# Query stacks rewritten in place by halves, gate-a tiles computed inside their own head pair, and five banks for filling

## The chip, the cores and the metric

The kernel runs on one core of a Trainium2 chip. The metric is the device time of one execution in microseconds (us). TensorE (PE) does the matrix products into eight PSUM banks, VectorE (DVE), ScalarE (ACT) and GpSimd (POOL) do the rest, and SyncE (SP) starts the loads.

## The reference

Two layers over 1088 token columns: 1024 of a prompt and 64 of a sample that continues a cache of 512 keys. Layer 0 runs attention over the 256 best keys of an indexer (8 heads of 64, two key/value heads) beside a short gated convolution. Layer 1 is a gated spatial mixer. Cut to the part that the change touches:

```python
q, k, v, ga, qi, ki, wi, gb, gc, xin, gz = _split(h @ w_in, EVEN_SPLITS)
...                      # top-k of the indexer's scores, masked logits
p = jax.nn.softmax(logits, axis=-1)
o = jnp.einsum('bqgrk,bqkgd->bqgrd', p, vg)
a_out = o * jax.nn.silu(ga)
...                      # short convolution: y
b_out = gb * y * jax.nn.silu(gz)
out = jnp.concatenate([a_out, b_out], axis=-1) @ w_out
```

## The kernel before

**Layout.** Activations lie with features on the partitions and the 1088 columns along the free axis. A projection tile is 128 output features: three chunks of columns (`CHUNKS`, 364, 364 and 360), each 24 matmuls (8 input tiles, times high by high, low by high and high by low parts), so 72 matmuls. A weight tile is loaded into one of two ring slots and split into a rounded high part by ACT (L238) and a low part by POOL (L239); `fetch()` starts this for the next tile when a tile begins, and the slot comes free when the tile before has been used.

**Attention of layer 0.** The eight heads are four pairs `t` = 0 to 3; `self.q[:, t, :]` holds a pair's queries and is overwritten by its output. For each pair `pair_stack` (L691) writes two query stacks of 128 partitions (high parts on one half by ACT, L698, low parts on the other by POOL, L699), whole, into tiles that are allocated anew for each pair. Then `attend` (L711) handles the blocks of 128 queries in the order of `ORDER`: block b has 128 x (b + 1) keys. Blocks 0 and 1 use a constant mask; the others use `bias`, which `mask` (L593 to L607) writes on DVE just before the attention. `softmax` computes logits in chunks of at most 512 keys (PE L620), adds the mask and takes the extremum (DVE L622), Exp (ACT L625), reciprocal (DVE L626) and division (POOL L627). `weighted` transposes the probabilities (PE L650), splits them into high and low parts (ACT L276, DVE L277) and multiplies them with the values (PE L658), in groups of two key blocks; the result goes back to q (ACT L662, DVE L722). `attend_sample` does the same for the 64 sample columns (L727, L732). Logits use PSUM banks of tag lg (three), transposes pt (two), sums av (one).

**Filling.** The projections that are left at that point are done as filling, one matmul per step: Q tiles 1 to 3, GB tiles 0 to 3 (product on DVE, L894), GA tiles 0 to 3 (gate a). `steps` (L250) is the generator, with the two banks of tag pj. The first `BEFORE` = 435 steps stand ahead of the attention. After that `pace` (L200) adds steps behind a matmul of the attention: `RATE` gives the number after a chunk of logits, after a group of weighted sums and after a group of transposes. A step may not be issued before the matmul that it was added behind. A GA tile waits until its pair is done (`self.done <= t`, L922); until then a step does nothing. So GA0 fills pair 1, GA1 pair 2, GA2 pair 3, and GA3 stands behind the last pair. `gate_a` copies a chunk to SBUF (L909), applies Silu to the whole tile after the third (L911) and multiplies it into q on POOL (L912); for t = 3 it does so chunk by chunk (L905, L906).

**Order.** Each engine runs its own queue in order. The order in the queues is made when the program is built, by a planner that follows the program's text where it can and lets later, ready instructions go ahead (`schedule_with_timeline_sim=True`). Afterwards q and bo are split into `ah` and `al` by chunks of columns (`OUT_CHUNKS`), and `out_projection` runs 8 tiles of 24 matmuls for each chunk, through `product`. The weights of its first two tiles use the two ring slots; the others get memory that attention has used.

Of the kernel before, what the change touches and what calls it, by code (L numbers as in the profile page):

```python
# [17 lines left out]
P = 128  # L18
# [17 lines left out]
NCH = 3  # L36
CW = 448


# [44 lines left out]
SPANS = [slice(min(COL[j] for j in g[0]), max(COL[j] for j in g[0]) + 1) for g in GROUPS]  # L84
ORDER = [(0, 1, 2, 3, 4, 5, 6, 7)] + [(7, 0, 6, 1, 5, 2, 4, 3)] * 3


BEFORE = 435
RATE = ((1, 1, 2),) * 4

# [7 lines left out]
class Trunk:  # L98
# [150 lines left out]

    def steps(self, w, evac, chunks=range(NCH), n=2, tag="pj"):  # L250

        hi, lo = w
        k = 0
        for c in chunks:
            a, b = CHUNKS[c]
            ps = self.bank(tag, "pj")[:, 0:b - a]
            for kt in range(KT):
                for i, (wt, at) in enumerate(((hi, self.ah), (hi, self.al), (lo, self.ah))):
                    if k and k % n == 0:
                        yield  # L260
                    k += 1
                    self.nc.tensor.matmul(ps, wt[:, kt, :], at[:, kt, a:b], start=kt == 0 and i == 0,  # L262
                                          stop=kt == KT - 1 and i == 2)
            evac(c, ps)
# [425 lines left out]

    def pair_stack(self, pool, t):  # L691

        nc = self.nc
        st = [pool.tile([P, TC], F32R, tag=f"qst{e}", name="qst") for e in range(2)]
        for a, b in ((0, 512), (512, TC)):
            for e in range(2):
                x, h, l = self.q[64 * e:64 * e + 64, t, a:b], slice(64 * e, 64 * e + 64), slice(64 - 64 * e, P - 64 * e)
                nc.scalar.activation(st[e][h, a:b], x, AF.Copy)  # L698
                nc.gpsimd.tensor_sub(st[e][l, a:b], x, st[e][h, a:b])  # L699
        return st  # L700

# [8 lines left out]

    def attend(self, pool, st, t, b):  # L711
        n = P * (b + 1)
# [10 lines left out]

    def attend_sample(self, pool, st, t):
        both = pool.tile([P, P], F32R, tag="qs", name="qs", bufs=1)
# [36 lines left out]
    def layer0(self):  # L762
# [41 lines left out]
        with ExitStack() as es:  # L804
# [74 lines left out]
            with self.pool("attn", "right") as ap:  # L879
# [8 lines left out]
                ap.tile([P, 512], F32R, tag="pth", name="place", bufs=2)  # L888
                for e in range(2):
                    ap.tile([P, TC], F32R, tag=f"qst{e}", name="place")  # L890

# [7 lines left out]
                def gate_a(t):  # L899
                    def evac(c, ps):  # L900
                        if c == 0:
                            ga[:] = [ap.tile([P, TC], F32, tag="ga", name="ga")]
                        g, q = ga[0], self.q[:, t, :]
                        if t == 3:
                            nc.scalar.activation(g[:, cols(c)], ps, AF.Silu)  # L905
                            nc.vector.tensor_mul(q[:, cols(c)], q[:, cols(c)], g[:, cols(c)])  # L906
                            return

                        nc.scalar.activation(g[:, cols(c)], ps, AF.Copy)  # L909
                        if c == NCH - 1:  # L910
                            nc.scalar.activation(g, g, AF.Silu)  # L911
                            nc.gpsimd.tensor_mul(q, q, g)  # L912
                    return evac

                evacs = {Q_: lambda t: into(self.q[:, t, :]), GB: gate_b, GA: gate_a}
                left = list(ATTN_TILES)
                self.done = 0

                def tiles():
                    while left:  # L920
                        kind, t = left[0]
                        while kind == GA and self.done <= t:  # L922
                            yield
                        key, w = ahead.pop(0)
                        assert key == (kind, t)
                        fetch()
                        yield from self.steps(w, evacs[kind](t), n=1)
                        left.pop(0)
                        yield

                self.side = tiles()
                for _ in range(BEFORE):
                    next(self.side)
                for t in range(4):
                    while (Q_, t) in left:
                        next(self.side)
                    self.rate = RATE[t]
                    st = self.pair_stack(ap, t)
                    for b in ORDER[t]:
                        self.attend(ap, st, t, b)  # L940
                    if t == 0:
                        self.sample_keys(ap)
                    self.attend_sample(ap, st, t)
                    self.done = t + 1
# [3 lines left out]
            for chunk in OUT_CHUNKS:  # L948
                s = slice(*chunk)
                for t in range(4):  # L950
                    for k, src in ((4 + t, self.bo), (t, self.q)):
                        self.split(self.ah[:, k, s], self.al[:, k, s], src[:, t, s])

# [7 lines left out]
    def out_projection(self, l, ws, after):  # L961
# [4 lines left out]
        for c in range(NCH):  # L966
# [4 lines left out]
            for t in range(KT):  # L971
                ps = self.bank(tags[0], "op")
                tags = tags[1:] + tags[:1]
                self.product(ps[:, 0:w], ws[t], a0, b0)
                for j, a, b in self.spans(c):
# [245 lines left out]
```

## Time and profile before

| | us |
|---|---|
| median of 3 runs | 1156.94 (1156.66 to 1160.60) |
| the profiled execution | 1157.27 |
| its span on the core | 1155.5 |
| filling without attention, DVE at top-k and masks | 344.8 to 424.8 |
| pairs 0 to 3 (first logits to the last write of the sample's columns) | 424.8, 481.9, 530.3, 581.3, 632.9 |
| output projection of layer 0 and layer 1 | from 634.8 |

Page and views name instructions by engine, line and tile. A busy PE includes matmuls that overlap, so a matmul's cost is read from the distance of starts; PEclk is the granted share of the TensorE clock, whose two levels are 2.4 and 1.2 GHz.

### The profile page before, as it was taken

Reading aid. Unit: us, or ns where it says so; the run is one execution under the profiler, and the core shown is the slowest. Engines: PE = TensorE matmul, PEld = TensorE weight load, DVE = VectorE, ACT = ScalarE, POOL = GpSimd, SP = SyncE. Lnnn points to the kernel's source line nnn. Section 1 sums busy time; section 2 is a strip of 40 time slices with the busy share of each in tenths; the row PEclk is TensorE's granted clock in tenths of the full one; section 3 lists DMA queues with packets and bytes.
Section 4 is the critical chain, followed back from the end, with each engine's and each line's share of the span. In section 5 each row is a group of like instructions: output and inputs, shape, how many; then the busy total and the mean of one; then the engine's idle time right before and its main releaser. Section 6 shows DMA issues by size and latency. Waiting matters only on the chain.

```text
span 1155.5 us, 18886 instructions
## 1 busy us (share of the span) xinstructions
PE 1100.1 (95%) x7255; PEld 1051.7 (91%) x7255; DVE 670.9 (58%) x1657; ACT 516.8 (45%) x976; POOL 442.6 (38%) x454
## 2 busy tenths in 40 slices
PE   4899999999999979999898999999999999999997
PEld 4789689999999968888797999999999999999996
DVE  5712799998886998776666424411186064247134
ACT  5233686856777147777757313511221211135111
POOL 2633223466547165354523136521133211154222
PEclk9999999999999989998999999999999999999999
DMA  9746411211101110000000801011112111131012
GB/s 362 305 156 215 179 29 56 91 40 38 37 19 56 37 46 10 20 1 19 19 1 19 281 2 40 35 55 37 37 57 82 37 37 37 38 109 37 1 65 91
DMA packets 26074, 81.84 MB, mean 71 GB/s; under 512 B 3072, under 2 KB 9984, under 8 KB 23552
## 3 DMA queue, kind: packets, MB, share of 16 engines
q1 hardware_dynamic: 25984, 80.63, 19.8%
q8 instruction: 57, 0.93, 0.3%
q14 instruction: 33, 0.27, 0.1%
HBM read 74.50 MB, written 6.12 MB: 70 GB/s over the span
## 4 chain that ended last, share of the span: by engine, by line
PE 79%; DVE 8%; ACT 5%; issue 3%; POOL 2%; DMA 2%; SPq 0%; POOLq 0%; DVEq 0%; ACTq 0%
PE pj L247 40%; PE op L247 16%; PE pj L262 8%; PE av L658 3%; PE p_ps L650 2%; PE logit_ps L620 2%; PE ada_ps L153 2%; PE score_ps L427 1%; PE sgu_ps L1036 1%; PE first L318 1%; DVE cum L604 1%; PE score_ps L428 1%; POOL w_lo L239 1%; POOL hf L329 1%; ACT S L625 1%
## 5 line engine op out<-in xcount | busy, mean ns | idle before, releaser
L247 PE MATMUL pj<-ah,w_hi 128*128 128x364 f32 (+1 forms) x984 | 326.0, 331 | 1.0 <-ACT w_hi L238 1.0
L247 PE MATMUL pj<-al,w_hi 128*128 128x364 f32 (+1 forms) x984 | 323.8, 329 | 0.0
L247 PE MATMUL pj<-ah,w_lo 128*128 128x364 f32 (+1 forms) x984 | 323.1, 329 | 0.0
L239 POOL TENSOR_TENSOR w_lo<-w_raw,w_hi 128x1024 fp32r<-128x1024 f32 x63 | 159.1, 2527 | 351.2 <-ACT w_hi L238 350.8
L247 PEld LDWEIGHTS pj<-ah,w_hi 128*128 128x128 f32 x984 | 185.0, 188 | 2.0 <-ACT w_hi L238 1.3
L247 PEld LDWEIGHTS pj<-ah,w_lo 128*128 128x128 f32 x984 | 184.8, 188 | 0.3 <-issue 0.2
L247 PEld LDWEIGHTS pj<-al,w_hi 128*128 128x128 f32 x984 | 185.1, 188 | 0.0
L238 ACT ACTIVATE w_hi<-w_raw 128x1024 fp32r<-128x1024 f32 x69 | 72.9, 1058 | 135.7 <-PE pj L247 83.2
L247 PE MATMUL op<-ah,w_lo 128*128 128x448 f32 (+2 forms) x384 | 126.5, 330 | 3.0 <-POOL w_lo L239 3.0
L247 PE MATMUL op<-ah,w_hi 128*128 128x448 f32 (+2 forms) x384 | 127.1, 331 | 0.9 <-ACT ah L276 0.5
L247 PE MATMUL op<-al,w_hi 128*128 128x448 f32 (+2 forms) x384 | 126.4, 329 | 0.7 <-DVE al L277 0.7
L528 DVE TENSOR_SCALAR_CACHE_REDUCE cum<-S,cand 128x512 bf16<-128x512 f32 (+5 forms) x142 | 119.1, 838 | 2.0
L262 PE MATMUL pj<-ah,w_hi 128*128 128x364 f32 (+1 forms) x288 | 96.0, 333 | 6.6 <-DVE bo L894 5.6
L262 PE MATMUL pj<-al,w_hi 128*128 128x364 f32 (+1 forms) x288 | 96.4, 335 | 0.0
L262 PE MATMUL pj<-ah,w_lo 128*128 128x364 f32 (+1 forms) x288 | 95.7, 332 | 0.0
L976 DVE SCALAR_TENSOR_TENSOR x<-op,mod,x 128x192 f32<-128x192 f32 (+2 forms) x64 | 30.4, 497 | 104.9 <-PE op L247 102.5
L555 ACT ACTIVATE junk<-S,cand 128x896 bf16<-128x896 f32 (+2 forms) x78 | 77.7, 996 | 24.3 <-DVE m L558 20.5
L627 POOL TENSOR_SCALAR S<-S,sm 128x384 f32<-128x384 f32 (+8 forms) x68 | 50.4, 748 | 87.2 <-DVE sm L626 64.9
L247 PEld LDWEIGHTS op<-ah,w_lo 128*128 128x128 f32 x384 | 73.0, 190 | 5.5 <-POOL w_lo L239 3.3
L247 PEld LDWEIGHTS op<-ah,w_hi 128*128 128x128 f32 x384 | 73.0, 190 | 3.5 <-ACT ah L276 0.9
L247 PEld LDWEIGHTS op<-al,w_hi 128*128 128x128 f32 x384 | 73.0, 190 | 3.3 <-DVE al L277 1.1
L984 POOL TENSOR_TENSOR acc<-acc,sq 128x448 f32<-128x448 f32 (+2 forms) x40 | 39.2, 979 | 94.4 <-ACT sq L982 93.6
(242 smaller groups left out, 2001.3 us busy)
## 6 DMA issues: line engine op xcount, KB each, us to landing
w_raw<-in_w SPq DMA_DIRECT2D x53, 512.0 KB, 3.4
ada<-in_ada_w SPq DMA_DIRECT2D x19, 1024.0 KB, 9.1
w_raw<-in_wo SPq DMA_DIRECT2D x16, 512.0 KB, 3.5
x<-in_x SPq DMA_DIRECT2D x8, 544.0 KB, 6.6
bo<-in_ada_w SPq DMA_DIRECT2D x4, 1024.0 KB, 6.9
x<-in_x SPq DMA_DIRECT2D x1, 1792.0 KB, 9.5
out_y<-x SPq DMA_DIRECT2D x1, 1792.0 KB, 6.6
x<-in_x SPq DMA_DIRECT2D x1, 1536.0 KB, 9.4
```

Source lines behind the costliest of these rows:

```text
L153: nc.tensor.matmul(pt[32 * g:32 * g + 32, 0:P], self.cs[:, kt, :], raw(kt)[:, g * P:(g + 1) * P], start=kt == 0, stop=kt == KT - 1, tile_p ...
L238: nc.scalar.activation(hi, raw, AF.Copy)
L239: (nc.gpsimd if lo_eng == "pool" else nc.vector).tensor_sub(lo, raw, hi)
L247: last = self.nc.tensor.matmul(ps, wt[:, kt, :], at[:, kt, c0:c1], start=n == 0, stop=n == len(mms) - 1)
L262: self.nc.tensor.matmul(ps, wt[:, kt, :], at[:, kt, a:b], start=kt == 0 and i == 0, stop=kt == KT - 1 and i == 2)
L528: V.tensor_scalar(junks[0][:, 0:SW[j]], self.S[:, span(j)], thr, 0.0, op0=OP.is_lt, op1=OP.add, accum_out=col(cv, j))
L555: nc.scalar.activation(junks[1][:, 0:SW[j]], self.S[:, span(j)], AF.Sign, scale=-1.0, bias=col(cand, j), accum_out=col(cv, j))
L620: mm = nc.tensor.matmul(pt[:, 0:w], lhs, keys[i][:, g, s], start=i == 0, stop=i == 1)
L627: nc.gpsimd.tensor_scalar(p, p, st[:, 3:4], 0.0, op0=OP.mult, op1=OP.add)
L658: mm = nc.tensor.matmul(av[:, 0:m], self.vs[0:r, vbase + j, g, :], t[0:r, o:o + m], start=j == 0 and i == 0, stop=j == nj - 1 and i == 1)
L976: nc.vector.scalar_tensor_tensor(x[:, t, a:b], ps[:, a:b], self.mod[l][:, 16 + t, j:j + 1], x[:, t, a:b], op0=OP.mult, op1=OP.add)
L984: nc.gpsimd.tensor_add(acc, acc, sq)
```

## The change

Three edits, and some order with them. (1) The two query stacks are allocated once (`self.st`). `stack_half` writes one half of the columns (0 to 512, or 512 to 1088) of both; the first half of pair t + 1 is written after the first block of pair t's second half, its second half after the first block of pair t + 1. `ORDER` is split accordingly, and the sample ("s") takes a place in the second half. (2) A GA tile may start when the pair before is done, so GA t fills pair t. It is always copied out by chunks, Silu follows on the whole tile, and the product with q comes after the pair's last block, on POOL for t < 3, on DVE in three column chunks for t = 3. Pair 0's rates become (2, 2, 3). (3) During the first 435 steps the filling goes round five banks (two pj, three lg); from then on it uses pj. The output projection of layer 0 takes the bo tiles before the q tiles (`OUT_KTS`), and the splits follow that order.

```diff
+OUT_KTS = (4, 5, 6, 7, 0, 1, 2, 3)
...
-ORDER = [(0, 1, 2, 3, 4, 5, 6, 7)] + [(7, 0, 6, 1, 5, 2, 4, 3)] * 3
+HALVES = ((0, 512), (512, TC))
+ORDER = [((0, 1, 2, 3), (4, 5, 6, 7, "s"))] + [((3, 0, 2, 1), ("s", 7, 4, 6, 5))] * 3
...
-RATE = ((1, 1, 2),) * 4
+RATE = ((2, 2, 3), *((1, 1, 2),) * 3)
...
-    def steps(self, w, evac, chunks=range(NCH), n=2, tag="pj"):
+    def steps(self, w, evac, chunks=range(NCH), n=2, tag=None):
...
-            ps = self.bank(tag, "pj")[:, 0:b - a]
+            if tag is None:
+                self.tags = self.tags[1:] + self.tags[:1]
+            ps = self.bank(tag or self.tags[-1], "pj")[:, 0:b - a]
...
-    def pair_stack(self, pool, t):
-        nc = self.nc
-        st = [pool.tile([P, TC], F32R, tag=f"qst{e}", name="qst") for e in range(2)]
-        for a, b in ((0, 512), (512, TC)):
-            for e in range(2):
-                x, h, l = self.q[64 * e:64 * e + 64, t, a:b], slice(64 * e, 64 * e + 64), slice(64 - 64 * e, P - 64 * e)
-                nc.scalar.activation(st[e][h, a:b], x, AF.Copy)
-                nc.gpsimd.tensor_sub(st[e][l, a:b], x, st[e][h, a:b])
-        return st
+    def stack_half(self, t, half):
+        nc = self.nc
+        a, b = HALVES[half]
+        for e in range(2):
+            x, h, l = self.q[64 * e:64 * e + 64, t, a:b], slice(64 * e, 64 * e + 64), slice(64 - 64 * e, P - 64 * e)
+            nc.scalar.activation(self.st[e][h, a:b], x, AF.Copy)
+            nc.gpsimd.tensor_sub(self.st[e][l, a:b], x, self.st[e][h, a:b])
...
-                for e in range(2):
-                    ap.tile([P, TC], F32R, tag=f"qst{e}", name="place")
+                self.st = [ap.tile([P, TC], F32R, name=f"qst{e}") for e in range(2)]
...
-                        if t == 3:
-                            nc.scalar.activation(g[:, cols(c)], ps, AF.Silu)
-                            nc.vector.tensor_mul(q[:, cols(c)], q[:, cols(c)], g[:, cols(c)])
-                            return
                         nc.scalar.activation(g[:, cols(c)], ps, AF.Copy)
                         if c == NCH - 1:
                             nc.scalar.activation(g, g, AF.Silu)
-                            nc.gpsimd.tensor_mul(q, q, g)
...
-                        while kind == GA and self.done <= t:
+                        while kind == GA and self.done < t:
...
+                self.tags = ["pj", "pj", "lg", "lg", "lg"]
                 for _ in range(BEFORE):
                     next(self.side)
+                self.tags = ["pj"]
+                self.stack_half(0, 0)
+                self.stack_half(0, 1)
                 for t in range(4):
-                    while (Q_, t) in left:
+                    self.rate = RATE[t]
+                    for half in range(2):
+                        for n, b in enumerate(ORDER[t][half]):
+                            if t == 0 and b == "s":
+                                self.sample_keys(ap)
+                            self.attend(ap, t, b)
+                            if n == 0 and (half or t):
+                                if half and t < 3:
+                                    self.stack_half(t + 1, 0)
+                                elif not half:
+                                    self.stack_half(t, 1)
+                    while (GA, t) in left:
                         next(self.side)
-                    self.rate = RATE[t]
-                    st = self.pair_stack(ap, t)
-                    for b in ORDER[t]:
-                        self.attend(ap, st, t, b)
-                    if t == 0:
-                        self.sample_keys(ap)
-                    self.attend_sample(ap, st, t)
+                    q = self.q[:, t, :]
+                    if t < 3:
+                        nc.gpsimd.tensor_mul(q, q, ga[0])
+                    else:
+                        for c in range(NCH):
+                            s = slice(*OUT_CHUNKS[c])
+                            nc.vector.tensor_mul(q[:, s], q[:, s], ga[0][:, s])
                     self.done = t + 1
...
-                for t in range(4):
-                    for k, src in ((4 + t, self.bo), (t, self.q)):
-                        self.split(self.ah[:, k, s], self.al[:, k, s], src[:, t, s])
+                for k in OUT_KTS:
+                    src = self.q if k < 4 else self.bo
+                    self.split(self.ah[:, k, s], self.al[:, k, s], src[:, k % 4, s])
...
-                self.product(ps[:, 0:w], ws[t], a0, b0)
+                self.product(ps[:, 0:w], ws[t], a0, b0, range(KT) if l else OUT_KTS)
```

## Rows read from the trace of the kernel before

**Rows 1.** The page, part 1: busy us (share of the span) and instructions

```profile
PE 1100.1 (95%) x7255; PEld 1051.7 (91%) x7255; DVE 670.9 (58%) x1657; ACT 516.8 (45%) x976; POOL 442.6 (38%) x454
```

**Rows 2.** Windows: length, busy us of PE, PEld, DVE, ACT, POOL; PEclk, DMA, GB/s

```profile
408.40:424.80 16.40, 10.83 (x54) 10.18 (x53) 16.40 (x14) 0.00 (x1) 9.60 (x5) 0.90 0.12 40
424.80:433.00 8.20, 6.02 (x29) 4.88 (x27) 5.76 (x30) 8.05 (x24) 5.84 (x8) 0.79 0.27 82
433.00:468.00 35.00, 34.27 (x229) 31.43 (x228) 28.05 (x84) 23.96 (x49) 17.40 (x19) 1.00 0.03 9
468.00:482.00 14.00, 12.37 (x77) 9.76 (x77) 10.94 (x42) 11.06 (x26) 8.25 (x9) 1.00 0.11 38
482.00:517.00 35.00, 34.00 (x239) 32.50 (x240) 26.83 (x87) 25.49 (x57) 15.14 (x18) 1.00 0.01 1
517.00:532.00 15.00, 12.76 (x53) 10.20 (x53) 8.27 (x27) 10.72 (x21) 7.70 (x6) 0.66 0.12 37
532.00:567.50 35.50, 34.91 (x236) 32.35 (x235) 25.88 (x88) 25.98 (x58) 15.18 (x17) 1.00 0.00 1
567.50:583.20 15.70, 11.71 (x53) 10.20 (x53) 7.22 (x24) 10.62 (x20) 7.48 (x7) 0.67 0.11 34
583.20:615.00 31.80, 31.56 (x222) 30.31 (x221) 20.35 (x63) 19.24 (x44) 6.69 (x9) 1.00 0.00 1
615.00:626.60 11.60, 10.60 (x71) 10.31 (x70) 8.21 (x18) 11.47 (x26) 4.95 (x2) 1.00 0.14 47
626.60:638.00 11.40, 7.53 (x33) 6.20 (x32) 10.40 (x21) 6.74 (x16) 4.94 (x1) 0.85 0.18 56
```

**Rows 3.** The chain that ended last, in order of time: start, us, what

```profile
344.93 34.43 PE pj L262 x207
...
634.82 47.11 PE op L247 x228
```

**Rows 4.** Windows of line L262 (filling) alone: PE busy and matmuls, then PEld

```profile
424.80:482.00 57.20, 17.42 (x78) 12.41 (x76) 0.97 0.08 27
...
517.00:532.00 15.00, 1.42 (x4) 1.02 (x5) 0.66 0.12 37
...
603.40:626.60 23.20, 16.95 (x93) 15.15 (x93) 1.00 0.07 23
```

**Rows 5.** Waits of PE, 400 to 640 us: total us, times, longest

```profile
PE pj L262 <- DVE bo L894: 5.6, 2, 3.3
...
PE logit_ps L620 <- POOL qst L699: 0.9, 1, 0.9
```

**Rows 6.** Timeline of DVE and POOL, 404 to 430 us: start, us, instruction, count

```profile
407.04 2.49 DVE L607 TENSOR_SCALAR bias<-bias 128x768 bf16<-128x768 bf16 x1
...
422.58 0.40 DVE L607 TENSOR_SCALAR bias<-bias 128x1024 bf16<-128x1024 bf16 x1
...
425.51 0.28 DVE L622 CUSTOM_DVE_ANT_0 S<-logit_ps,corner 128x128 f32<-128x128 f32 x1
...
405.89 3.42 POOL L239 TENSOR_TENSOR w_lo<-w_raw,w_hi 128x1024 fp32r<-128x1024 f32 x1 [9.13 <-ACT w_hi L238]
...
426.88 2.36 POOL L239 TENSOR_TENSOR w_lo<-w_raw,w_hi 128x1024 fp32r<-128x1024 f32 x1
```

**Rows 7.** Timeline of ACT at the start of attention and in pair 1's end

```profile
425.76 1.04 ACT L238 ACTIVATE w_hi<-w_raw 128x1024 fp32r<-128x1024 f32 x1
426.82 1.28 ACT L625 ACT_TABLE_LOAD   x1
...
518.66 1.28 ACT L911 ACT_TABLE_LOAD   x1
519.95 1.11 ACT L911 ACTIVATE ga<-ga 128x1088 f32<-128x1088 f32 x1
```

**Rows 8.** Timeline of DVE and POOL at the end of pair 3

```profile
632.97 2.19 DVE L906 TENSOR_TENSOR q<-q,ga 128x360 f32<-128x360 f32 x1
...
629.83 4.94 POOL L239 TENSOR_TENSOR w_lo<-w_raw,w_hi 128x1024 fp32r<-128x1024 f32 x1 [9.42 <-ACT w_hi L238]
```

More of the change, by code (lines that the diff above doesn't have):

```diff
@@ L709, in sample_keys, with attend @@
                 self.nc.scalar.activation(self.kc[i][:, g, PAST:NS], self.kp[i][:, g, SO:SO + DEC], AF.Copy)
-    def attend(self, pool, st, t, b):
+    def attend(self, pool, t, b):
+        if b == "s":
+            return self.attend_sample(pool, t)
+        st = self.st
         n = P * (b + 1)
@@ L722, in attend, with attend_sample @@
             self.nc.vector.tensor_add(self.q[64 * e:64 * e + 64, t, c], av[0:64, s], low[:, s])
-    def attend_sample(self, pool, st, t):
+    def attend_sample(self, pool, t):
+        st = self.st
         both = pool.tile([P, P], F32R, tag="qs", name="qs", bufs=1)
@@ L902, in evac @@
                             ga[:] = [ap.tile([P, TC], F32, tag="ga", name="ga")]
-                        g, q = ga[0], self.q[:, t, :]
-                        if t == 3:
-                            nc.scalar.activation(g[:, cols(c)], ps, AF.Silu)
-                            nc.vector.tensor_mul(q[:, cols(c)], q[:, cols(c)], g[:, cols(c)])
-                            return
+                        g = ga[0]
                         nc.scalar.activation(g[:, cols(c)], ps, AF.Copy)
```

## Prediction

> **What bounds the kernel now.** I read the page's first part, which puts TensorE (PE) at 95% of the span [rows 1], then cut the stretch that the change touches, 408.4 to 638 us, into windows [rows 2]. Before it, filling runs without a gap: 207 matmuls in 34.43 us, 0.1663 us each, so a tile of 72 is 12.0 us [rows 3]. In the windows two things cost PE time: idle time (window less PE busy) and time at the lower clock level, 1.2 GHz (2 x (1 - PEclk) x window, half of which is lost). By that measure the losses are: last masks 5.6 + 1.6 = 7.2 us; start of attention 2.2 + 1.7 = 3.9; body of pair 0 0.7; end of pair 0 1.6; body of pair 1 1.0; end of pair 1 2.2 + 5.1 = 7.3; end of pair 2 4.0 + 5.2 = 9.2; end of pair 3 1.0 + 3.9 + 1.7 = 6.6 [rows 2]. The bodies of pairs 2 and 3 lose 0.6 and 0.2, so they repeat pair 1's. All of it is about 38 us.
>
> The reader should see that a pair loses almost nothing while it has fill and most of its loss where fill has run out: in 517 to 532 us only 4 fill matmuls run, in the whole of pair 0 78, and 93 lie in 603.4 to 626.6 us, where the gate-a tile of pair 3 has come behind the attention [rows 4]. **The change moves PE work and removes none**, so its most is those 38 us.
>
> **Five banks for filling.** Before, filling has two PSUM banks, and PE waits 5.6 us in two stalls for DVE to clear one [rows 5]. With five banks these go, and PE ends its 435 matmuls at about 425 - 7 = 418 us. But DVE is busy for 16.40 of the 16.40 us of that window [rows 2], and the first attention operation on DVE starts at 425.51, right behind the last mask [rows 6]. What is late next is DVE, so the 5.6 us buy nothing unless the planner puts the first logits among the masks. Two small effects remain. The weight conversion on ACT at 425.76 (1.04 us) stands right before the Exp table load at 426.82 [rows 7]; it waits for PE to leave a weight slot, so it moves forward: -0.8. Its second half on POOL (2.4 us) then falls among the masks, where POOL work has hurt: L607 took 2.49 us while POOL converted a weight until 409.31, and 0.40 us later [rows 6]. That would cost 0 to +2.1, less what it no longer disturbs at 427. Also, the 19th chunk (three matmuls of GB3) falls on a bank of tag lg and keeps one of the three that the first logits need; no row shows logits on two banks, and I bound it by 0 and the 2.2 us of idle time at the start, which is itself mostly a wait for a bank. **Value -1**, the 0.8 rounded, because the other two are small against their bounds if the conversion merely changes its place; from -4.7 (all of the 3.9 at the start, and 0.8) to +4.3 (2.1 + 2.2).
>
> The Trainium skill, "SBUF — State Buffer", section "Who interferes with whom", on the port pair that VectorE and GpSimd share, says that the instruction that comes second is blocked until the first one ends. L607 agrees: it ended 0.2 us after POOL's operation. By that rule alone the moved conversion would cost the masks up to its own 2.4 us, and the part would come to +1.6.
>
> **Stacks by halves.** The same 16 ACT and 16 POOL operations run. The next pair's first half is written while this pair is in its second, on columns that nobody reads any more. Queued behind them are Exp and the copies of p on ACT, and the softmax divisions on POOL. What PE visibly waited for a stack is 0.9 us [rows 5], once in three pair changes, because the logits run ahead of the weighted sums. The bodies of pairs 1 to 3 lose 1.8 us together. **Value -1**, from -1.8 to +2 (a 1.3 us POOL operation ahead of a division, some of the time in three pairs; estimated).
>
> **Gate-a in its own pair: what pair 0 pays.** A pair has 26 chunks of logits, 21 groups of transposes that pace and 22 groups of weighted sums. At rates (1, 1, 2) that is 26 + 22 + 42 = 90 steps, at (2, 2, 3) 52 + 44 + 63 = 159. Pair 0 now has 69 + 72 = 141 matmuls instead of 69: **+12.0 us** of PE. Of its idle time, 0.7 us in the body can be covered: **-0.7**. At its end there is now a Silu between Exps. Such a place shows two table loads of 1.28 us and a Silu of 1.11 us, 3.67 us on ACT [rows 7], ahead of the copies of p that PE's weighted sums wait for. The ends of pairs 1 and 2, which have this, lose 7.3 and 9.2 us; pair 0, which has not, loses 1.6, so the Silu's place costs between 0 and 8.25 - 1.6 = +6.6. In pair 0 the fill now runs out in block 7, with 1.4 groups of that block and the sample left, against 5.3 groups in pairs 1 and 2: nearer the middle than the top. **Value +3.**
>
> The Trainium skill, "ScalarE: Activation LUTs", section "Table sets: the hidden batching unit" and its rules, gives a switch of tables about 2.7 us and advises doing all calls of one set together, which speaks against this edit. The loads here took 1.28 us. With the page's figure the pair of loads would be 5.4 us instead of 2.6, and this term about 6.
>
> **What the tail gains.** GA3's 72 matmuls leave the tail: **-12.0 us**. They now take the place in pair 3 that GA2's had, as GA2's take GA1's in pair 2. Where the stall goes: GA3's Silu now stands at the end of pair 3 with no GA fill behind it. As cover there are the first two tiles of the output projection, whose weights sit in the two ring slots: 24 matmuls each at 47.11 / 228 = 0.207 us [rows 3], 9.9 us. Their order now begins with the bo tiles, which are ready. The end of the last pair also sheds the weight conversion that now runs earlier: at 629.83 it took 4.94 us on POOL, the last gate product beside it took 2.19 us [rows 8]. Later weights still need memory that attention frees, so a seam stays. Of the 6.6 us I leave 4: **value -2.6**, from -6.6 (all covered) to +2.6 (it goes like pair 2's end, 9.2).
>
> **Order of blocks in pairs 1 and 2.** The 72 matmuls run out in block 6 instead of block 4; after that 4.7 groups of weighted sums stay instead of 5.3, and those of the next pair's block 3 follow. The burst on ACT is the same. POOL's product q x gate (2.5 us) waits for the end of the pair, and the next gate chunk needs its buffer only 24 steps later, which is after the change of pairs. **Value -1 each, -2**; bounds from -5.7 and -7.6 (both end like pair 0) to +2 each (three quarters of a group more stall; an estimate from 9.2 us over 5.3 groups).
>
> **Sum**: -1 - 1 + 12.0 - 0.7 + 3 - 12.0 - 2.6 - 2 = -4.3. The profiled execution took 1157.27 us (span 1155.5, 1.8 around it): 1157.3 - 4.3 = 1153.0. The median shown is 0.3 lower, 1156.94, so I say **1153**.
>
> **Rivals.**
> (a) The pair ends heal. The early stack and the small blocks at the head of the next pair give PE work where it now runs dry, and the clock stays at its upper level. For it: pair 0 ends at PEclk 1.00 with a loss of 1.6, and half of what pairs 1 and 2 lose is the lower clock. Against it: the next pair's fill still cannot start before that pair, and ACT's burst stays. Price: -13.3 for both ends instead of -2, so 1153 - 11.3, about **1142**; with one end healed 1148.
> (b) Slower: a Silu without fill at four pair ends instead of two. Place: ACT's queue at the ends of pairs 0 and 3. Price: pair 0 +6.6 instead of +3, pair 3's end 9.2 + 3.9 idle at the seam = 13.1 instead of 4, so 1153 + 3.6 + 9.1, about **1166**. It decides where the first two output tiles do not get onto PE before the last weighted sum. For it: before, PE had only 9 matmuls of them ahead of the last weighted sums. Against it: then GA3 was still in the way, and the splits came late for that.
> (c) It does nothing: fill added to pair 0 is paid in full, fill taken from the tail is given back at the seam, and pairs 1 and 2 repeat. +12 - 12, **1157**.
>
> **How the numbers follow.** Chances: forecast 0.40 (own range 1149 to 1157), (a) 0.30, (c) 0.12, (b) 0.18. A measurement of this kernel can tell about 0.5%, 5.8 us, from no change, which makes the borders 1151.2 and 1162.7. Faster: all of (a) and a good quarter of the forecast, 0.42. Slower: (b), 0.18. Same: 0.40. The range runs from (a)'s time, 1142, to 1164, which takes in the first half of (b); the bounds of the unknown costs reach further only if several end together. Forecast alone: 1149 to 1157.
>
> **What would show each step.** Banks: no wait of L262 for L894 before 425, and yet the first L622 near 425. Stacks: no PE wait for qst. Pair 0: about 150 fill matmuls, PE idle under 1 us in the body, a table load near its end; the value is wrong if PEclk falls there. Tail: no L262 after the last Exp, more than 9 matmuls of op ahead of the last weighted sum, and under 4 us lost from there to the steady op stream. Ends of pairs 1 and 2: PEclk 0.66 again, or 1.00 for (a). The forecast is wrong if the masks end well before 425, or if pair 0 grows by less than 8 us or more than 18.

## The result, and the profile of the changed kernel

The changed kernel took **1167.84 us** (median of 4 runs, 1166.56 to 1168.74), the kernel before 1157.59 beside it (median of 4, 1156.66 to 1160.60): ratio 1.0083, 95% interval 1.0062 to 1.0105. The forecast was 1153. The profiled execution took 1166.56, with a span of 1164.9 us against 1155.5, 9.4 more.

To see where they lie I cut both traces into stages at events that both kernels have: first matmul of the filling without attention, first softmax operation on DVE (L622 before, L628 now), last addition into q of each pair on DVE (L722 or L732 before, L730 or L741 now), the 61st matmul of the output projection, and its last one in layer 0. The cuts are rounded, so a difference can be off by 0.1.

| stage, us | before | changed | difference | forecast |
|---|---|---|---|---|
| filling and masks, to the first softmax | 80.7 | 84.6 | +3.9 | -1 |
| pair 0 | 56.6 | 70.0 | +13.4 | +14.3 |
| pair 1 | 48.2 | 49.2 | +1.0 | -3 for |
| pair 2 | 51.0 | 47.9 | -3.1 | both |
| pair 3 and the seam, to the 61st output matmul | 64.9 | 58.8 | -6.1 | -14.6 |
| the rest of the output projection of layer 0 | 85.8 | 85.8 | 0.0 | 0 |

So pair 0 and pairs 1 and 2 came out near what was worked out. Two terms fail: the start by 4.9 us, the tail by 8.5. Together they are the 13.4 us between the forecast of -4.3 and the +9.1 of these rows.

**The start.** Windows of the changed kernel (columns as in [rows 2]), then PE's waits from 400 to 660 us (releaser, total us, times, longest):

```profile
408.40:417.10 8.70, 8.70 (x55) 8.70 (x53) 8.66 (x10) 0.25 (x1) 0.00 (x0) 1.00 0.22 75
417.10:429.50 12.40, 1.76 (x7) 1.01 (x6) 12.33 (x10) 3.89 (x9) 9.98 (x5) 0.60 0.13 42
429.50:437.00 7.50, 6.34 (x22) 5.35 (x22) 3.93 (x23) 5.79 (x17) 3.04 (x6) 0.53 0.07 20
```

```profile
PE logit_ps L626 <- DVE bo L902: 5.4, 1, 5.4
PE logit_ps L626 <- DVE sm L628: 5.3, 8, 2.4
PE logit_ps L626 <- POOL qst L705: 5.2, 1, 5.2
...
PE op L251 <- ACT w_hi L242: 3.5, 2, 3.2
PE av L664 <- DVE ptl L283: 2.7, 4, 1.8
```

The two stalls of [rows 5] are gone, and PE is through its 435 matmuls at 417.1 us instead of 424.6. It then stands for 10.6 us in two waits: the first logits wait 5.2 us for POOL's part of the query stack, the next 5.4 us for a bank of tag lg that a GB product still holds. DVE is busy throughout, and PE works on from 429.5 at a granted clock of 0.53. ACT, POOL and DVE there (start, us, instruction):

```profile
416.85 1.06 ACT L242 ACTIVATE w_hi<-w_raw 128x1024 fp32r<-128x1024 f32 x1 [10.93 <-PE pj L268]
417.82 2.68 ACT L704 ACTIVATE qst<-q 64x512 fp32r<-64x512 f32 x4
```

```profile
417.99 2.41 POOL L243 TENSOR_TENSOR w_lo<-w_raw,w_hi 128x1024 fp32r<-128x1024 f32 x1 [9.61 <-ACT w_hi L242]
420.47 7.80 POOL L705 TENSOR_TENSOR qst<-q,qst 64x512 fp32r<-64x512 f32 x4
```

```profile
393.00 0.53 DVE L902 TENSOR_TENSOR bo<-bo,pj 128x360 f32<-128x360 f32 x1 [1.42 <-PE pj L268]
...
418.23 3.25 DVE L612 SCALAR_TENSOR_TENSOR bias<-S,T,bias 128x1024 bf16<-128x1024 f32 x1
...
429.47 0.28 DVE L628 CUSTOM_DVE_ANT_0 S<-logit_ps,corner 128x128 f32<-128x128 f32 x1
```

The conversion of [rows 7] has moved forward as forecast, from 425.76 to 416.85. But in ACT's queue it moved past more than the Exp: the four writes of the first stack, which waited for nothing before and stood at 405.72, are now behind it at 417.82. Last, DVE begins the first softmax at 429.47 instead of 425.51 [rows 6].

**The ends of pairs 1 and 2**, in windows as long as those of [rows 2] for 517 and 567.5 us (0.66 and 0.67 there), and the end of pair 0:

```profile
482.00:501.50 19.50, 15.85 (x82) 13.76 (x81) 10.19 (x35) 13.84 (x24) 8.43 (x7) 0.74 0.08 28
537.00:552.00 15.00, 11.26 (x61) 9.26 (x61) 9.20 (x30) 12.27 (x24) 8.21 (x9) 0.89 0.11 35
585.00:600.70 15.70, 12.76 (x72) 10.55 (x71) 10.30 (x32) 12.90 (x23) 7.59 (x9) 0.89 0.10 34
```

By the prediction's measure (idle time, and what the lower clock takes) the ends lose 3.7 + 1.7 = 5.4 us instead of 7.3 and 2.9 + 1.7 = 4.7 instead of 9.2: the clock's part shrinks to a third, the idle part (6.2 us together before, 6.6 now) stays. At the end of pair 0 the clock now falls, which it did not before.

**The seam**, the stretch from the end of pair 3's attention to the steady output projection (columns as before; PE, then ACT):

```profile
628.00:655.40 27.40, 20.97 (x106) 17.94 (x105) 16.19 (x29) 14.82 (x27) 2.36 (x1) 0.88 0.29 95
```

```profile
638.28 0.58 PE L664 MATMUL av<-ptl,vs 128*128 128x256 f32 x1 [1.79 <-DVE ptl L283]
638.66 1.06 PE L656 MATMUL p_ps<-ident,S 128*128 128x128 f32 x4
639.37 0.72 PE L251 MATMUL op<-ah,w_lo 128*128 128x448 f32 x1
...
644.04 0.36 PE L251 MATMUL op<-ah,w_lo 128*128 128x448 f32 x1
644.24 0.60 PE L656 MATMUL p_ps<-ident,S 128*128 128x128 f32 x4
...
647.42 0.28 PE L664 MATMUL av<-ptl,vs 128*128 128x256 f32 x1
650.88 0.47 PE L251 MATMUL op<-ah,w_hi 128*128 128x448 f32 x1 [3.18 <-ACT w_hi L242]
```

```profile
649.36 0.52 ACT L282 ACTIVATE ah<-q 128x384 fp32r<-128x384 f32 x1 [1.24 <-DVE q L963]
649.79 1.99 ACT L242 ACTIVATE w_hi<-w_raw 128x1024 fp32r<-128x1024 f32 x2
```

All 48 output matmuls whose weights are there (two tiles of 24) run ahead of the last weighted sum, the first of them at 621.4 and 19 of them (639.37 to 644.24) in a block ahead of the last transposes. Then nothing is left: the last weighted sum at 647.42, DVE's addition and gate product, ACT's split of q at 649.36, and only behind it on ACT the weights of output tile 2, for which PE has waited 3.2 us.

### The profile page after: what moved, and what is told of

Same layout as the page of the kernel before. It is cut to its first block, busy times and chain, and to the rows that moved or that the text cites. A ratio compares the mean times of both kernels' runs of the same rounds, so it can differ in the third digit from the quotient of the medians.

```text
span 1164.9 us, 18890 instructions
## 1 busy us (share of the span) xinstructions
PE 1099.4 (94%) x7255; PEld 1051.2 (90%) x7255; DVE 673.3 (58%) x1657; ACT 522.4 (45%) x979; POOL 440.1 (38%) x454
## 4 chain that ended last, share of the span: by engine, by line
PE 82%; DVE 7%; ACT 4%; issue 3%; DMA 2%; POOL 2%; SPq 0%; POOLq 0%; DVEq 0%; ACTq 0%
PE pj L251 40%; PE op L251 16%; PE pj L268 10%; PE av L664 3%; PE logit_ps L626 2%; PE p_ps L656 2%; PE ada_ps L157 2%; PE score_ps L433 1%; PE sgu_ps L1056 1%; PE first L324 1%; DVE al L283 1%; DVE bias L612 1%; PE score_ps L434 1%; DMA x<-in_x 1%; DVE cum L610 1%
## 5 line engine op out<-in xcount | busy, mean ns | idle before, releaser
L243 POOL TENSOR_TENSOR w_lo<-w_raw,w_hi 128x1024 fp32r<-128x1024 f32 x63 | 156.4, 2483 | 350.8 <-ACT w_hi L242 350.5
L633 POOL TENSOR_SCALAR S<-S,sm 128x128 f32<-128x128 f32 (+8 forms) x68 | 51.0, 755 | 78.4 <-DVE sm L632 66.6
```

The costliest lines, as they stand in the source:

```text
L243: (nc.gpsimd if lo_eng == "pool" else nc.vector).tensor_sub(lo, raw, hi)
L633: nc.gpsimd.tensor_scalar(p, p, st[:, 3:4], 0.0, op0=OP.mult, op1=OP.add)
```

## Experiments: what each part is worth

Times are given as ratios to the kernel before, run on the same chip (0.1% is 1.16 us). The stage differences (to the kernel before, us, cut as above) come from the profiled execution of each. The stretch ahead of the first cut is left out; it varied by up to 2.6 us between executions.

| kernel | ratio (95%) | start | pair 0 | pair 1 | pair 2 | pair 3, seam | rest |
|---|---|---|---|---|---|---|---|
| changed | 1.0083 (1.0062 to 1.0105) | +3.9 | +13.4 | +1.0 | -3.1 | -6.1 | 0.0 |
| a_two_banks | 1.0035 (1.0017 to 1.0054) | 0.0 | +13.5 | +1.3 | -3.1 | -6.0 | 0.0 |
| b_five_banks | 1.0040 (1.0025 to 1.0055) | +3.8 | +0.7 | -0.1 | +1.1 | +0.8 | -0.5 |
| a_gate_late | 0.9997 (0.9985 to 1.0010) | +3.8 | +1.9 | +1.8 | -2.9 | -3.3 | -0.5 |
| b_gate_own_pair | 1.0017 (1.0003 to 1.0032) | 0.0 | +14.1 | +1.5 | 0.0 | -11.8 | +0.1 |
| b_stack_halves | 0.9988 (0.9976 to 1.0000) | +0.1 | +1.3 | +0.9 | -2.2 | +0.5 | -0.5 |

**Two banks again.**

```diff
-                self.tags = ["pj", "pj", "lg", "lg", "lg"]
                 for _ in range(BEFORE):
```

> The changed kernel with two banks for filling again (one line out), all else as changed. Theory 1 (three separate causes: the five banks cost about 4 us at the start of attention because a weight conversion gets ahead of the first query stack on ACT; gate-a in its own pair costs about 7 us at the seam behind pair 3 and 1 us in pair 0; stacks and order give back some 5 us at the ends of pairs 1 and 2): 1167.8 - 4 = 1164, the stretch 344 to 437 us loses 13 us of PE time instead of 17, and the first stack is on ACT near 406 us. Theory 2 (the gate-a part, a Silu without fill at pair ends, is the whole loss, and the banks are worth nothing or the 1 us forecast): 1167 to 1169.

1163.40 us, theory 1. The start is that of the kernel before, all else as changed.

**Five banks alone.** The kernel before, with the diff's edits to `steps` and `self.tags`.

> The kernel before with the five banks for filling alone. Theory 1: 1157.6 + 4 = 1161.6, first stack behind one more weight conversion on ACT, PE waiting for POOL's part of the stack and for DVE's product on a bank of tag lg. Theory 2, and the forecast's term: 1156.6 to 1157.6.

1163.30 us: the same loss in the other kernel, in the same stage. In these two kernels the five banks cost some 0.4 to 0.5%. In every kernel with five banks the start is some 3.5 to 4 us longer (2.0 in a_conv_late), but the ratios behind another output order differ by less (a_cover against a_two_cover below, 0.1%).

**Without the gate-a part.**

```diff
-                        while kind == GA and self.done < t:
+                        while kind == GA and self.done <= t:
...
-RATE = ((2, 2, 3), *((1, 1, 2),) * 3)
+RATE = ((1, 1, 2),) * 4
```

with product and Silu in `gate_a` as before.

> The changed kernel without its gate-a part (a gate-a tile again starts when its own pair is done, pair 0 at rates 1, 1, 2); stacks by halves, their order and five banks stay. Theory 1: 1157.6 + 4 - 5 = about 1157, with the ends of pairs 1 and 2 still at the upper clock for longer than before. Theory 2: 1156 to 1157 as well, but with the start of attention as before. Theory 3 (the ends of pairs 1 and 2 heal because the gate-a tiles end elsewhere, not by the stacks and the order): 1161 to 1162, the ends of both pairs again at half clock for about 10 us.

1158.44 us; theory 1, with the start 3.8 us longer, so theory 2 is out. Theory 3 is out too: pair 2 still gains 2.9 us, and both ends keep a granted clock of 0.89, against 0.66 and 0.67 in the kernel before:

```profile
528.00:543.00 15.00, 11.16 (x58) 9.08 (x58) 9.15 (x30) 12.51 (x24) 9.09 (x10) 0.89 0.11 36
576.00:591.70 15.70, 12.68 (x70) 10.34 (x69) 10.32 (x33) 12.71 (x23) 8.32 (x9) 0.89 0.10 35
```

**The gate-a part alone**, the kernel before with that edit the other way round.

> The kernel before with the gate-a part alone (a gate-a tile in its own pair, product behind the pair, pair 0 at rates 2, 2, 3). Theory 1: 1157.6 + 7 + 1 = about 1166, the loss at the seam. Theory 2: about 1168. Theory 3 (the gate-a part also heals the ends of pairs 1 and 2): about 1160.

1160.95 us: neither 1166 nor 1168. The number is theory 3's, about 1160, but not for its reason: pairs 1 and 2 are no shorter than before, and the clock at their ends still falls:

```profile
535.00:550.00 15.00, 12.14 (x61) 10.17 (x61) 7.50 (x24) 9.35 (x18) 5.59 (x6) 0.77 0.11 36
583.60:599.30 15.70, 11.72 (x54) 10.41 (x55) 7.04 (x25) 10.47 (x19) 6.79 (x7) 0.67 0.09 33
```

In the kernel before, the edit costs 0.17%, in the changed kernel 0.86% (1.0083 against 0.9997). Each time against the kernel without it, the edit costs pair 0 14.1 us here and 11.5 there (13.4 - 1.9), and the seam takes back 11.8 us here and only 2.8 there (6.1 - 3.3). So the failed tail is **no property of the gate-a part alone**, but of that part together with the other edits; what the new orders do in it is tried below.

**Stacks by halves alone**, with their order of blocks; two banks, gate-a late, splits and output tiles in the old order.

> The kernel before with the stacks by halves and their order of blocks alone (two banks, gate-a tiles a pair late, splits and output projection in the old order of tiles). Theory 1 (the parts add up, and this one is worth what the run without the gate-a part gains over the five banks alone): 0.5% faster than before, about 1154, with 3.4 us instead of 10.2 at half clock at the ends of pairs 1 and 2, and under 7 us lost from there to the steady output projection. Rival (the part gains only what the five banks lose, by starting the stacks late together): no difference from before.

1157.23 us, between the two: 0.12% instead of 0.5%, and the interval reaches 1. Pair 2 gains, pairs 0 and 1 lose some of it, and the seam gains nothing. What a_gate_late has beyond it in the seam is the third, small edit, the bo tiles first (see best_late below).

## Experiments: the start

**No lg bank held by the last chunk.** The 19th chunk, which the prediction had named, begins on a pj bank.

```diff
-                for _ in range(BEFORE):
+                for n in range(BEFORE):
+                    if n == 432:
+                        self.tags = ["pj"]
                     next(self.side)
-                self.tags = ["pj"]
```

> The changed kernel, five banks for the first 432 steps of filling only; the last three steps before the attention begin their chunk on a pj bank, so that no lg bank is held. If the held lg bank is what the five banks cost: 5 us faster than the changed kernel, 1.0035 of before. If it is the first stack, late behind a weight conversion on ACT, and POOL's work among the last masks: within 1.5 us of the changed kernel, 1.007 to 1.0085 of before, with the masks ending near 429 us again.

1167.51 us, ratio 1.0077 (1.0055 to 1.0098): not this chunk.

**The first stack ahead of the conversion.** `fetch` comes four steps later in the GB3 tile, and the conversion may not be issued before the stack:

```diff
-        nc.scalar.activation(hi, raw, AF.Copy)
+        if getattr(self, "laststack", None):
+            with self.tc.issue_after(self.laststack):
+                nc.scalar.activation(hi, raw, AF.Copy)
+            self.laststack = None
+        else:
+            nc.scalar.activation(hi, raw, AF.Copy)
```

> The changed kernel, five banks kept, but the weight conversion that is waiting for PE's slot near 417 us is issued behind the first stack on ACT (and so on POOL). Theory (the five banks cost 4.6 us because ACT holds the first stack back behind that conversion): the stack is written near 406 us, the masks end near 425, about 1163, 1.0035 to 1.004 of before. Rival (PE simply meets the masks earlier, and POOL's work costs the masks wherever it stands): 1.007 or more.

1166.78 us, ratio 1.0062 (1.0042 to 1.0083). The edit worked, the theory did not. ACT wrote the stack at 405.25, POOL was done with it at 416.48, but the start is still 3.7 us longer. The logits behind the first pair (PE's row) now wait for the bank alone, and for longer:

```profile
428.73 0.66 PE L632 MATMUL logit_ps<-kp,qst 128*128 128x128 f32 x2 [11.32 <-DVE bo L908]
```

The late stack was a wait in front of another that ends last anyway: DVE's queue, where masks and GB products stand ahead of the first softmax. What DVE did in the masks, by line (columns: count, busy us, mean ns, idle just before), for the kernel before, the changed one, and this one:

```profile
L606 DVE SCALAR_TENSOR_TENSOR bias<-S,T,bias 128x384 bf16<-128x384 f32 (+6 forms) x7 | 9.1, 1295 | 0.1
L607 DVE TENSOR_SCALAR bias<-bias 128x384 bf16<-128x384 bf16 (+6 forms) x7 | 5.5, 790 | 0.0
```

```profile
L612 DVE SCALAR_TENSOR_TENSOR bias<-S,T,bias 128x384 bf16<-128x384 f32 (+6 forms) x7 | 11.7, 1671 | 0.2
L613 DVE TENSOR_SCALAR bias<-bias 128x384 bf16<-128x384 bf16 (+6 forms) x7 | 5.0, 711 | 0.0
L902 DVE TENSOR_TENSOR bo<-bo,pj 128x364 f32<-128x364 f32 (+1 forms) x9 | 4.6, 515 | 1.4 <-PE pj L268 1.4
```

```profile
L618 DVE SCALAR_TENSOR_TENSOR bias<-S,T,bias 128x384 bf16<-128x384 f32 (+6 forms) x7 | 9.8, 1396 | 0.2
L619 DVE TENSOR_SCALAR bias<-bias 128x384 bf16<-128x384 bf16 (+6 forms) x7 | 7.1, 1019 | 0.0
```

The four longest mask lines (these two, the scan and L605) take 34.3 us before, 36.4 changed and 36.2 here. So 2.1 of the 3.9 us are masks that run longer, and 1.4 are DVE waiting at 391.6 for a chunk that PE had not finished. This wait stands there in all ten kernels with five banks and in none of the seven with two: in the kernel before, three mask instructions (391.50 to 393.46) stand ahead of the same GB product.

**The conversion behind the first Exp**, otherwise the same edit with the first Exp in the stack's place and `fetch` ten steps later instead of four.

> The changed kernel, five banks kept; the weight conversion of 417 us is issued behind the first Exp, on ACT and POOL, so that it stands behind the masks as in the kernel before, and the first stack is on time. Theory (five banks only turn PE's waits in the filling into one wait ahead of the first logits, and what they cost on top is POOL's conversion and stack beside the last masks): masks end near 425, PE waits 8 us from 417 to 425, 1.0035 to 1.005 of before, 3 to 5 us faster than the changed kernel. Rival (the lg banks that filling holds keep the first logits waiting behind DVE's products even with the masks done): first logits near 428 again, 1.006 or more.

1170.02 us, ratio 1.0089 (1.0068 to 1.0109): no faster than the changed kernel, and yet the part of the theory on POOL beside the masks holds. Without the conversion beside them the four mask lines take 34.6 us again and the start is 2.0 us longer than before instead of 3.9; the 1.4 us of waiting is still there. The time is lost behind it: pair 0 is 3.3 us longer than in the changed kernel, with the conversion now standing among the first Exps (ACT, 431.70, 1.04 us) and on POOL among the first divisions (432.82, 2.36 us). PE waited 9.7 us for the bank of the second logits; of the rival it is true that the wait is one for an lg bank, but its end moves with the masks.

## Experiments: the seam

| kernel | ratio (95%) | pair 3, seam | rest |
|---|---|---|---|
| a_old_out | 1.0047 (1.0030 to 1.0064) | -9.2 | -0.5 |
| a_sample_last | 1.0072 (1.0046 to 1.0099) | -7.9 | +0.1 |
| a_cover | 1.0008 (0.9996 to 1.0020) | -18.1 | +5.6 |
| a_two_cover | 0.9998 (0.9989 to 1.0007) | -18.1 | +6.4 |

**The old order of output tiles.**

```diff
-OUT_KTS = (4, 5, 6, 7, 0, 1, 2, 3)
+OUT_KTS = (4, 0, 5, 1, 6, 2, 7, 3)
...
-                self.product(ps[:, 0:w], ws[t], a0, b0, range(KT) if l else OUT_KTS)
+                self.product(ps[:, 0:w], ws[t], a0, b0)
```

> The changed kernel with the old order of tiles in the splits and in the output projection of layer 0 (the bo tiles no longer first). Theory A (output-projection matmuls get ahead of the last transposes because their bo part is ready early, and that delays the end of the last pair): 3 to 5 us faster than the changed kernel. Theory B (those matmuls are the only cover that the seam has): 2 to 4 us slower than the changed kernel.

1163.90 us, theory A: only 7 output matmuls instead of 19 now stand between the last two groups of transposes, and the seam is 3.1 us shorter.

**The sample last in pair 3.**

```diff
-ORDER = [...] + [((3, 0, 2, 1), ("s", 7, 4, 6, 5))] * 3
+ORDER = [...] + [((3, 0, 2, 1), ("s", 7, 4, 6, 5))] * 2 + [((3, 0, 2, 1), (7, 6, 5, 4, "s"))]
```

> The changed kernel with the second half of pair 3 in the order 7, 6, 5, 4, sample instead of sample, 7, 4, 6, 5. Theory 1 (the seam loses 15 us instead of 9 because the attention ends on a long block, whose last weighted sum, gate product, split and then the weight conversion of the third output tile follow one another with no matmuls left beside them): 4 to 6 us faster than the changed kernel, seam loss under 11. Rival (the seam is long because gate-a of pair 3 no longer covers it, whichever block is last): within 1.5 us of the changed kernel.

1166.07 us; 1.8 us in the seam, some 0.1% in the ratio, inside the intervals. Which block is last is at most a small part.

**More matmuls that need no later weights.** In the output projection of layer 0, tiles 0 and 1 of the first two chunks of columns come first:

```diff
-        for c in range(NCH):
+        heads = ((0, range(2)), (1, range(2)), (0, range(2, KT)), (1, range(2, KT)), (2, range(KT)))
+        for c, ts in heads if l == 0 else [(c, range(KT)) for c in range(NCH)]:
...
-            for t in range(KT):
+            for t in ts:
```

> The changed kernel with another order in the output projection of layer 0: tiles 0 and 1 of the first two chunks of columns come first, then tiles 2 to 7 of both, then the third chunk, so 96 matmuls instead of 48 need no later weights. If PE runs dry at the seam because only two tiles' weights are there (3.2 us wait for tile 2's high part, and the chain ahead of it): 3 to 5 us faster than the changed kernel, 1.004 to 1.0055 of before. If the chain from the last transposes on sets the seam: within 1.5 us of the changed kernel.

1160.72 us, more than expected: 0.75% off. The seam by itself is 12.0 us shorter; 5.5 come back in the rest, since matmuls were moved forward from there, so 6.5 are gained. PE's clock stays up through the whole stretch that had 0.88:

```profile
628.00:643.20 15.20, 14.04 (x89) 12.99 (x88) 11.61 (x22) 11.61 (x22) 2.38 (x1) 1.00 0.10 36
643.20:655.40 12.20, 10.09 (x57) 8.85 (x57) 4.17 (x8) 3.40 (x5) 0.00 (x0) 1.00 0.27 88
```

By the prediction's measure the two windows of this kernel lose 3.3 us, all of it idle time, where 628 to 655.4 of the changed kernel lost 6.4 idle and 3.3 by the clock. So more **work that could run** closes most of the seam: the chain of split and conversion at its end is as it was (652.11 and 652.54 on ACT), only with matmuls beside it. Of the 96, 88 run ahead of the last weighted sum, and a block of 16 still stands ahead of the last transposes; what PE waits for behind it is the split, not the weights:

```profile
652.69 0.62 PE L251 MATMUL op<-ah,w_hi 128*128 128x384 f32 x2 [1.88 <-ACT ah L282]
```

Whether the weights of tile 2, converted ahead of the split on ACT, would have done the same was not tried.

**Both repairs together**, two banks and this order.

> The changed kernel with two banks for filling and with the first two output tiles of two chunks of columns ahead of the later tiles: the two largest losses undone, stacks by halves and gate-a in its own pair kept. If start and seam are separate causes: 1.0035 + 1.0008 - 1.0083 = 0.996 of before, near 1155. If they share a cause: 1.0 or more.

1158.25 us: level with the kernel before, not 0.4% faster. By the stages the two do add up: those of a_two_banks sum to +5.7, of a_cover to +2.8, of the changed kernel to +9.1, which leaves -0.6 for both repairs together, and the stages here sum to +0.1. It is the ratios that do not add up; that of a_cover, 0.9 us, is below the sum of its own stages. Beside the groups of runs the kernel before had medians from 1157.59 to 1160.27 us, so sums of ratios are less sure than each interval says. Where the 0.3% between the ratios lies stays open.

## Experiments: a faster version

| kernel | ratio (95%) | start | pair 0 | pair 1 | pair 2 | pair 3, seam | rest |
|---|---|---|---|---|---|---|---|
| best_late | 0.9954 (0.9939 to 0.9969) | +1.2 | +0.3 | +0.3 | -3.1 | -3.5 | 0.0 |
| best_late_ahead | 0.9967 (0.9955 to 0.9979) | +3.7 | +0.1 | +0.3 | -3.0 | -3.7 | -0.4 |
| best_cover | 0.9947 (0.9932 to 0.9961) | +0.1 | +1.3 | +0.9 | -2.2 | -4.9 | +0.6 |

> The changed kernel without the gate-a part and without the five banks: stacks by halves, their order, and the bo tiles first. If the parts add up (no gate-a part: -10 us, two banks: -4.6): 0.9955 of before, about 1153.5. If the bo tiles first are worth nothing while gate-a tiles come a pair late: 0.9985, as the stacks by halves alone.

1153.64 us, as the sum says: **faster than both kernels**, by 0.46% against the one before. It is b_stack_halves with the bo tiles first and nothing else (`OUT_KTS` in splits and product), so that small edit is worth 0.34% here, as much as the seam alone changes (+0.5 to -3.5), while in the changed kernel it costs 0.36% (a_old_out). Here GA3's matmuls stand at the seam as cover, and 21 output matmuls instead of 9 run ahead of the last weighted sum on top of them. There the output matmuls were all the cover there was, and a_old_out shows that part of them was spent too early.

> The changed kernel without the gate-a part, five banks kept, the first stack ahead of the waiting weight conversion. If the late stack is the whole cost of the five banks: as the same kernel with two banks, or up to 1 us faster, 0.9945 to 0.9955 of before. If the five banks cost by other ways: 0.9985 to 1.0.

1155.70 us, between the two: with five banks the start is 3.7 us longer also here.

> The version without gate-a part and without five banks (0.9954 of before) with the same new order of the output tiles. If that seam already has cover enough from gate-a's own matmuls: 0.9945 to 0.996. If the seam still lacks some: 0.9915 to 0.994, 2 to 4 us faster than without it.

1152.97 us; the interval overlaps best_late's, so no gain is shown. PE is busy for all of the 14 us from 628 to 642, where best_late has 13.64:

```profile
628.00:642.00 14.00, 14.00 (x76) 13.27 (x75) 13.01 (x24) 7.39 (x15) 3.38 (x1) 1.00 0.43 138
```

## Why the prediction was wrong

**Five banks: -1 forecast, +3.9 measured.** What was right: the two stalls go, PE is through at 417.1 (418 forecast), and this buys nothing because DVE's masks end last (in the kernel before a GB product, at 425.07, stood between them and the first softmax, so the queue that counts is masks and products). What failed is the step "Two small effects remain", in three places. First, POOL's half of the conversion was bounded by "0 to +2.1"; the value taken was near 0, and measured was the upper bound, 2.1 us of longer mask lines, most of which went again when the conversion was taken out (a_conv_late). The Trainium skill, "SBUF — State Buffer", section "Who interferes with whom", says that on the port pair that VectorE and GpSimd share, the instruction that comes second is held until the first has ended. By it the prediction's sum for this part was +1.6. The trace agrees: POOL's conversion began at 417.99 and ended at 420.40, L612 began at 418.23 and took 3.25 us, where the same instruction took 1.27 us before (below). Second, with five banks one GB product stands in DVE's queue 1.4 us before PE is ready for it. Nothing in the rows of before showed that, and why the planner puts it there is not shown; it lies 17 us ahead of the first of the two stalls (408.8), so it is not the missing stall itself. Third, I asked what the conversion moves past on ACT and named the Exp only, not the four stack writes; that cost a visible wait but, by a_stack_ahead, some 0.2% of time, inside the intervals. I bounded the bank by the 19th chunk; without it on an lg bank the start is as long (a_five_pj), and what the logits wait for is the product of the 18th, at 428.81 in DVE's queue.

**Stacks by halves and order: -3 forecast, -2.1 measured.** Near in size in this kernel; alone (b_stack_halves) pairs 0 to 2 sum to 0.0, so the size is in part luck. (The bound of +2 there is 1.3 by its own figures, three quarters of 9.2 / 5.3; nothing hung on it.) The ends heal as to the clock and not as to idle time, so rival (a), with its 13.3 us off both ends, came true for less than half (6.4 us, by the windows above), and most of that is not seen in the stages.

**Pair 0: +14.3 forecast, +13.4 measured** (+14.1 alone). The sum holds, its parts less so. The end behaves as the upper bound: by the prediction's measure 482 to 499.5 us loses some 8 us against 1.6, 6 more and not 3, and its sign against the value, a fall of PEclk, is there. What paid for it is that the body had more room than the 0.7 us of idle time. An estimate from the distance of starts (each matmul counted at the lower quartile of its line and shape) has PE lose some 11 us in pair 0 of either kernel, although the end now loses 6 more: a matmul that waits for the one before it counts as busy, and 68 more filling matmuls (143 instead of 75) use that time. The measure was too small, and two errors met; that the sum came out is luck.

**Tail: -14.6 forecast, -6.1 measured.** The first term, 12 us for 72 matmuls, fits: in b_gate_own_pair the seam gives back 11.8. The step that failed is "As cover there are the first two tiles of the output projection", 9.9 us, after which 4 us of loss were left. By the prediction's measure 628 to 655.4 us loses 6.4 + 3.3 = 9.7, and pair 3 up to 628 another 2.5. The 48 matmuls did run there, and were not enough: all had run before the chain that they were to cover had ended. I had counted how much work was ready but neither whether it would last nor where the queue would put it. The bo-first order, which I had counted as a help, is what let 19 of them, not 7, go ahead of the last transposes (a_old_out, 3.1 us), and double the cover gives back 6.5 us (a_cover). Whether the two add up was not tried.

**Rival (b), 1166**, is nearest in time, and its price for the seam (+9.1) is near the 8.5 found. But its condition did not come about: the output matmuls did get ahead of the last weighted sum. And its other half, +3.6 more in pair 0, did not happen; the five banks filled its place in the sum. So its time came near by luck, with the place right and the mechanism not. Rival (c)'s "fill taken from the tail is given back at the seam" is true of half of it.

## What to carry to other kernels

Count as cover not all the work that is ready, but what of it is still unissued when the last chain runs. More of it helped here (6.5 us), and making it ready earlier can spend it too early: the same edit was worth 4 us with other work at the seam and cost 4 without. Before removing a stall on an engine that is not the last to finish, list what else is then moved forward in each queue and what it runs beside. Edits that are made together should be tried apart: here one gained a little, two lost, and the one that looked most harmful cost a fifth as much by itself.

## What was not expected of the hardware

How much a mask operation suffers beside POOL: L612 on 128x1024 took 3.25 us there. The same instruction of the kernel before, with POOL idle:

```profile
420.06 1.27 DVE L606 SCALAR_TENSOR_TENSOR bias<-S,T,bias 128x1024 bf16<-128x1024 f32 x1
```

After standing for 10.6 us PE worked at the lower level, 1.2 GHz, up to 436.6 us, 7 us beyond its return to work; in the kernel before, with 5.6 us in two stalls and 2.2 us of idle time at the start of attention, it was two spells of 3.4 us between 412 and 434 us.
